# Input projections of a hybrid block's mixer in one stage of seven-product pairs, with results through DRAM and the recurrent branch's output projection beside attention

## The chip, the cores and the metric

The kernel runs on one core of a Trainium2 chip. The metric is the device time in microseconds of one execution. A core has a matrix engine (PE, with its own weight loads, PEld), a vector engine (DVE), a scalar engine (ACT), a general engine (POOL) and a sync engine (SP) that mostly issues DMAs. All of them share an on-chip memory (SBUF); PE writes to PSUM banks, from which DVE and ACT read; DMA queues move data to and from the memory outside (DRAM).

## The reference

One layer with width 1024, sequence 1024, batch 1: a half feed-forward (ffn1), a mixer, another half feed-forward (ffn2), each behind a norm and a modulation computed from a vector `c`. The change is in the mixer.

```python
def mixer(h, w_in, rel_bias, conv_w, conv_b, lru_wa, lru_ba, lru_wx, lru_bx, lru_lambda,
          w_att_o, w_rec_o, w_out):
    proj = h @ w_in
    q, k, v, xr, yr, g_att, g_rec = jnp.split(proj, idx, axis=-1)   # widths 512 x 3, 1024 x 4
    att = chunked_attention(q, k, v, rel_bias) @ w_att_o            # 8 heads of 64, own chunk + 8 before
    xr = causal_depthwise_conv(xr, conv_w, conv_b)                  # width 4
    rec = (rg_lru(xr, lru_wa, lru_ba, lru_wx, lru_bx, lru_lambda) * jax.nn.gelu(yr)) @ w_rec_o
    merged = jax.nn.sigmoid(g_att) * att + jax.nn.sigmoid(g_rec) * rec
    return merged @ w_out
```

`rg_lru` computes two gates by block-diagonal products, from them a decay `a` and an input `u`, and the recurrence h(t) = a(t) h(t-1) + u(t) along the sequence.

## The kernel before, in words

Everything is kept transposed: 128 channels on the partitions, 1024 positions along the free axis. A float32 product is made of three matmuls on split operands (high by high, high by low, low by high), so each operand is first cut into a high half (a cast on ACT) and a low half (a subtraction on DVE, or on POOL); `split` does that for weights. A projection of 128 columns over 1024 inputs and 1024 positions takes 48 matmuls of 512 columns.

In ffn1 and ffn2 most pairs of column groups (gate and up) go through seven products instead of eight, in the manner of Strassen and Winograd: the eight half-size products of two 128-column groups, each over two halves of the inputs, become seven over mixed operands, 84 matmuls instead of 96. `mix` makes the mixed weights: sums on POOL (L611), the high half on ACT (L623), the low half on DVE (L624). Sums of the moving operand are made once (`sum_step`, `differences`). `block` runs the products in the order 1, 2, 6, 5, 7, 3, 4 into three banks (`psX`, `psY`, `psZ`); after each, ACT copies a bank or DVE adds it (`vec`, L643).

The mixer has four phases after ffn1.
- `lru_phase`: for each of eight groups b, direct products for xr and yr, the convolution (three DVE operations, L1042), the GELU of yr, the gates' matmuls, the decay, one POOL product (L1090), the scan on DVE (L1091), and the split of the result, which stays in SBUF as `rec_h`, `rec_l`. Its matmuls are followed by those of the next group, in an order that the framework's scheduler sets.
- `rec_out_phase`: for each n the gate `gr` and the product with `w_rec_o`; the result goes to DRAM (`part`). Beside it runs background work (`bg`): the modulation vector's columns for later, summed on DVE from 512 KB pieces of `w_ada` (L203).
- `att_phase`: PE's order is fixed by hand, unit by unit (4 head pairs p x 2 heads x 8 query blocks, 64 units). For each unit come `scores` (sc), the softmax on DVE and ACT (L1344 maximum, L1347 its negation, L1348 exp, L1349 reciprocal, L1350 scaling), the transposes (`ptr`), their split (`tt`, ACT L1362, DVE L1363), and the product with v (`pvo`), gathered by L1386 to L1390. Between these PE gets `filler`: the projections of the next pair's q and k, half of v, and the gate `ga`, 192 matmuls of 512 columns (or their worth) per pair, dealt out in proportion to `SHARE` by the width of the unit's window. `GATES` says how many of the `ga` columns each pair takes.
- `merge_phase`: the product with `w_att_o`, the two gated branches added. Then `out_phase`.

## Time and profile before

| | us |
|---|---|
| Median of 3 runs | 2229.1 (2227.11 to 2230.41) |
| The profiled execution | 2231.5 |
| Its span, first to last instruction | 2229.6 |
| Beside it (2231.5 - 2229.6) | 1.9 |

In the profile a line number such as L624 is that of the kernel file. A row of a group has the engine, the operation, output and inputs by the program's names, shapes and a count; then either "busy us, mean ns" and the idle time before it with what ended that, or the least, median and greatest duration in ns. The table of stages has, for a window of time, its length and then for PE, PEld, DVE, ACT and POOL the busy time with the number of instructions, the granted clock of PE as a share of full speed, the busy share of the DMA engines and what they moved. In the list of waits a row says which engine and line waited for which, for how long in all, how many times, and the longest. In this execution ffn1's pairs run until about 700 us, the recurrence beside x and y to 946, gates and rec out to 1104, q, k and half of v to 1151, attention to 1422, the merge to 1466.

### The profile page before, as it was taken

Reading aid. Unit: us, or ns where it says so; the run is one execution under the profiler, and the core shown is the slowest. Engines: PE = TensorE matmul, PEld = TensorE weight load, DVE = VectorE, ACT = ScalarE, POOL = GpSimd, SP = SyncE. Lnnn points to the kernel's source line nnn. Section 1 sums busy time; section 2 is a strip of 40 time slices with the busy share of each in tenths; the row PEclk is TensorE's granted clock in tenths of the full one; section 3 lists DMA queues with packets and bytes.
Section 4 is the critical chain, followed back from the end, with each engine's and each line's share of the span. In section 5 each row is a group of like instructions: output and inputs, shape, how many; then the busy total and the mean of one; then the engine's idle time right before and its main releaser. Section 6 shows DMA issues by size and latency. Waiting matters only on the chain. (4 is left out here: it accounts for less than half of the span.)

```text
span 2229.6 us, 26752 instructions
## 1 busy us (share of the span) xinstructions
PE 2156.7 (97%) x9963; PEld 1785.0 (80%) x9963; DVE 1332.4 (60%) x1696; ACT 1016.1 (46%) x1567; POOL 758.2 (34%) x538
## 2 busy tenths in 40 slices
PE   5999999999999999999999999999999999999998
PEld 3878788888877788888898988887788788888877
DVE  6686676558356677655336666545866564544456
ACT  3533333334446678721147777436443333334443
POOL 3458885422104111100021120005658793522102
PEclk9999999999999999999999999999999999999999
DMA  9437674459575111166412011464357653348374
GB/s 294 113 120 268 226 272 153 151 183 336 182 240 184 50 50 42 57 221 221 155 40 68 26 55 54 146 199 142 110 181 263 229 209 126 113 155 275 117 230 176
DMA packets 269595, 358.36 MB, mean 161 GB/s; under 512 B 16625, under 2 KB 178585, under 8 KB 269465
## 3 DMA queue, kind: packets, MB, share of 16 engines
q1 hardware_dynamic: 256680, 310.48, 43.0%
q10 hardware_dynamic: 12784, 46.18, 5.4%
q8 instruction: 78, 1.28, 0.2%
q14 instruction: 53, 0.43, 0.1%
HBM read 265.37 MB, written 94.37 MB: 161 GB/s over the span
## 5 line engine op out<-in xcount | busy, mean ns | idle before, releaser
L624 DVE TENSOR_TENSOR wm<-raw,wm 128x512 fp32r<-128x512 f32 x152 | 161.0, 1063 | 165.3 <-ACT wm L623 162.5
L143 ACT CAST dh<-rawd 128x1024 fp32r<-128x1024 f32 x154 | 161.3, 1053 | 212.1 <-PE pv L882 67.0
L144 DVE TENSOR_TENSOR dh<-rawd,dh 128x1024 fp32r<-128x1024 f32 x130 | 161.9, 1250 | 153.4 <-ACT dh L143 145.3
L455 PE MATMUL pj<-hh,wl 128*128 128x512 f32 x576 | 228.3, 396 | 6.3 <-DVE wl L144 4.1
L454 PE MATMUL pj<-hl,wh 128*128 128x512 f32 x576 | 228.5, 397 | 5.7 <-DVE hl L336 5.7
L453 PE MATMUL pj<-hh,wh 128*128 128x512 f32 x576 | 230.9, 401 | 2.8 <-ACT h L344 1.9
L882 PE MATMUL px<-dh,dh 128*128 128x512 f32 x608 | 187.8, 390 | 1.7 <-DVE dh L144 1.7
L882 PE MATMUL pv<-dh,dh 128*128 128x512 f32 x528 | 164.3, 393 | 3.0 <-DVE dh L144 3.0
L325 POOL TENSOR_SCALAR rstd<-rstd 128x1 f32<-128x1 f32 x47 | 31.7, 675 | 392.5 <-ACT junk L324 390.9
L144 POOL TENSOR_TENSOR wl<-raw,wh 128x1024 fp32r<-128x1024 f32 x25 | 61.1, 2450 | 297.8 <-ACT wh L143 252.0
L143 ACT CAST wh<-raw 128x1024 fp32r<-128x1024 f32 (+1 forms) x86 | 86.7, 1010 | 144.9 <-DMA raw<-in_w_in_dram 41.8
L820 POOL TENSOR_TENSOR act<-act,act 128x512 f32<-128x512 f32 x54 | 87.5, 1620 | 158.9 <-DMA act<-act 89.1
L882 PE MATMUL px<-dh 128*128 128x512 f32 x352 | 137.9, 392 | 0.0
L455 PEld LDWEIGHTS pj<-hh,wl 128*128 128x128 f32 x576 | 110.2, 191 | 31.2 <-DVE wl L144 5.7
L882 PEld LDWEIGHTS px<-dh,dh 128*128 128x128 f32 x608 | 113.8, 188 | 26.5 <-DVE dh L144 3.0
L454 PEld LDWEIGHTS pj<-hl,wh 128*128 128x128 f32 x576 | 110.0, 191 | 29.9 <-DVE hl L336 7.6
L453 PEld LDWEIGHTS pj<-hh,wh 128*128 128x128 f32 x576 | 110.2, 191 | 26.2 <-ACT h L344 2.3
L144 DVE TENSOR_TENSOR wl<-raw,wh 128x1024 fp32r<-128x1024 f32 (+1 forms) x61 | 73.9, 1212 | 84.8 <-ACT wh L143 84.8
L633 PE MATMUL psX<-hh,wm 128*128 128x512 f32 x296 | 116.4, 393 | 4.3 <-ACT mixes L656 4.3
L882 PEld LDWEIGHTS pv<-dh,dh 128*128 128x128 f32 x528 | 99.5, 189 | 25.0 <-DVE dh L144 4.3
L633 PE MATMUL psX<-hs,wm 128*128 128x512 f32 x296 | 115.9, 391 | 1.6 <-ACT mixes L649 1.4
L623 ACT CAST wm<-raw 128x512 fp32r<-128x512 f32 x152 | 92.6, 613 | 52.1 <-POOL raw L611 52.0
(311 smaller groups left out, 5783.9 us busy)
## 6 DMA issues: line engine op xcount, KB each, us to landing
rawa<-in_w_ada_dram SPq DMA_DIRECT2D x56, 512.0 KB, 4.5
raw<-in_ffn_w_gu_dram SPq DMA_DIRECT2D x49, 512.0 KB, 4.7
rawd<-acts SPq DMA_DIRECT2D x88, 256.0 KB, 4.3
rawd<-downs SPq DMA_DIRECT2D x88, 256.0 KB, 4.1
raw<-in_w_in_dram SPq DMA_DIRECT2D x44, 512.0 KB, 4.0
sr<-in_ffn_w_gu_dram SPq DMA_DIRECT2D x39, 512.0 KB, 6.3
act<-act SPq DMA_DIRECT2D x37, 512.0 KB, 5.1
acts<-act ACTq DMA_DIRECT2D x36, 512.0 KB, 3.6
```

What stands on the lines that cost most here:

```text
L143: nc.scalar.copy(hi, raw)
L144: (eng or nc.vector).tensor_tensor(lo, raw, hi.bitcast(F32), op=ALU.subtract)
L325: nc.gpsimd.tensor_scalar(r, r, eps, None, op0=ALU.add)
L453: nc.tensor.matmul(dst, wh[:, kk, :], xhk[:, sl], start=first, stop=False)
L454: nc.tensor.matmul(dst, wh[:, kk, :], xlk[:, sl], start=False, stop=False)
L455: nc.tensor.matmul(dst, wl[:, kk, :], xhk[:, sl], start=False, stop=last)
L623: nc.scalar.copy(t[:, 0], src)
L624: nc.vector.tensor_tensor(t[:, 1], src, t[:, 0].bitcast(F32), op=ALU.subtract)
L633: nc.tensor.matmul(dst, t[:, 0, kk, :], xh, start=first and kk == 0, stop=False, skip_group_check=True)
L820: nc.gpsimd.tensor_tensor(o, p, q, op=op)
L882: nc.tensor.matmul(dst, a_[:, 0, tk], w_[:, 1, :], start=first and n == 0, stop=last and n == 2, skip_group_check=True,)
```

## The change: what it does

`seven` is cut out of `ffn`, with its sums, mixes and products unchanged, so that the mixer can use it. `lru_phase`, `rec_specs`, `rec_out_phase`, and the projections inside `att_phase` go; a `mixer_phase` takes their place, which computes all input projections. Its order is written by hand for all four compute engines. It starts with two direct `gr` columns and v, beside which the sums and the first mixes are made. Then come 19 blocks of seven products: xy0, gr, xy1, gr, xy2, gr, xy3, ga, xy4, ga, xy5, ga, xy6, ga, xy7, and q with k for the four head pairs. After each product, `after` makes one mix of the next block, and takes one step of the recurrence (`lru_steps`, a generator) and one of the gates' or q and k's conversion (`gate_steps`, `qk_steps`), and after three of the seven one step of the background work.

```diff
+        def block(n, after):
+            ...
+            run(1, chain, True)
+            nc.scalar.copy(u, chain)
+            after(1)
+            run(2, b2, True)
+            vec(u, b2, u)
+            after(2)
+            run(6, chain, False)
+            nc.scalar.copy(v, chain)
+            after(6)
+            b3 = bank("psZ")
+            run(5, b3, True)
+            nc.scalar.copy(pp, b3)
+            after(5)
+            run(7, chain, False)
+            vec(pp, chain, pp)
+            after(7)
+            run(3, b3, False)
+            vec(v, b3, v)
+            after(3)
+            run(4, chain, False)
+            if kind in ("gr", "ga"):
+                nc.scalar.activation(low, chain, AF.Tanh, scale=0.5)
+            else:
+                nc.scalar.copy(low, chain)
+            after(4)
+            return row0, row1
...
+        def lru_steps(b, xr, y):
...
+            nc.scalar.activation(q, q, AF.Sqrt)
+            yield
+            nc.gpsimd.tensor_tensor(ti, ti, q, op=ALU.mult)
+            yield
+            nc.vector.tensor_tensor_scan(q, a, ti, 0.0, op0=ALU.mult, op1=ALU.add)
+            nc.vector.tensor_tensor(q, q, g, op=ALU.mult)
+            rh = t4("rh", F32R)
+            nc.scalar.copy(rh, q)
+            yield
+            nc.vector.tensor_tensor(q.bitcast(F32R), q, rh.bitcast(F32), op=ALU.subtract)
+            yield
+            for i, src in enumerate((rh.bitcast(F32), q)):
+                nc.sync.dma_start(rec_d[i, b * P : (b + 1) * P, :], src)
+            yield
...
+                def after(i):
+                    sv.mix(n + 1, i)
+                    for q in (heavy, light):
+                        if q and next(q[0], BANK) is BANK:
+                            q.pop(0)
+                    if i in (2, 5, 3):
+                        bg(1)
```

The results go to DRAM: the recurrence's high and low halves (`rec_d`, 8 MB), q and k (`qk_d`), v (`v_d`), and the gates (`tgr`, `tga`). `att_phase` loads them again with DMAs issued by POOL, and its filler is now the product with `w_rec_o`, two column groups (96 matmuls) per head pair. `merge_phase` loads its gate from DRAM as before, for all columns.

```diff
+            def load_rec():
+                hi = [hpool.tile([P, S], F32R, tag="h", bufs=16, name=nm("rh")) for _ in range(KB)]
+                lo = [hpool.tile([P, S], F32R, tag="h", bufs=16, name=nm("rl")) for _ in range(KB)]
                 for k in range(KB):
+                    for i, t in enumerate((hi[k], lo[k])):
+                        nc.gpsimd.dma_start(t, rec_d[i, k * P : (k + 1) * P, :])
...
             def filler(p):
-                for kind, n in plan[p]:
-                    ...
+                load_qk(p + 1)
+                yield from rec_out(2 * p)
+                load_v(p)
+                yield from rec_out(2 * p + 1)
 
             with tc.manual_schedule(engines={PE_ENGINE}):
                 load_bias(0)
-                for _ in qk(0, qkt):
-                    pass
+                load_qk(0)
+                load_rec()
+                load_v(-1)
                 pe_next = scores(units[0])
-                for _ in vproj(0, vts):
-                    pass
...
-                    rate = (weight_of(p) - (LEFT if p == 3 else 0.0)) / tot
+                    rate = (96.0 - (LEFT if p == 3 else 0.0)) / tot
```

How this stands in the engines' programs, at three places. A number behind a name is that of the buffer. First DVE around one scan of the recurrence. Before (`xc` convolution, `wl` the low half of a weight, `xcl` and `rl` low halves, `g` the GELU):

```order
L1089 SCALAR_TENSOR_TENSOR ti_6016<-ti_6016,xc_5694 128x1024
L1042 SCALAR_TENSOR_TENSOR xc_5987<-xr_5986,colsB,xc_5987 128x1021
L1087 SCALAR_TENSOR_TENSOR q_6097<-q_6097,tr_6015 128x1024
L1051 TENSOR_TENSOR xcl_5996<-xc_5987,xch_5995 128x512
L1051 TENSOR_TENSOR xcl_6000<-xc_5987,xch_5999 128x512
L1091 SCALAR_TENSOR_TENSOR q_6097<-a_6096,ti_6016 128x1024
L144 TENSOR_TENSOR wl_6191<-raw_6188,wh_6190 128x1024
L1064 TENSOR_SCALAR g_6090<-g_6090 128x1024
L1092 TENSOR_TENSOR a_6096<-q_6097,g_5905 128x1024
```

The same stretch of a scan in the change (`wm` low halves of the next block's mixes, `acc` the background sums, `row` with a `ps` bank the block's own sums):

```order
L1211 SCALAR_TENSOR_TENSOR ti_6561<-ti_6561,xc_6454 128x1024
L1110 TENSOR_TENSOR row_1006_6605<-psY_6608,row_1006_6605 128x512
L558 TENSOR_TENSOR wm_6648<-rawm_6601,wm_6648 128x512
L202 SCALAR_TENSOR_TENSOR acc_6328<-rawa_6573,c_act,acc_6328 128x1024
L558 TENSOR_TENSOR wm_6671<-rawm_6601,wm_6671 128x512
L1215 SCALAR_TENSOR_TENSOR q_6629<-q_6629,tr_6560 128x1024
L558 TENSOR_TENSOR wm_6691<-wsum_6622,wm_6691 128x512
L202 SCALAR_TENSOR_TENSOR acc_6328<-rawa_6655,c_act,acc_6328 128x1024
L1110 TENSOR_TENSOR row_1007_6606<-psX_6607,row_1007_6606 128x512
L558 TENSOR_TENSOR wm_6711<-rawm_6603,wm_6711 128x512
L1220 SCALAR_TENSOR_TENSOR q_6629<-a_6628,ti_6561 128x1024
L1221 TENSOR_TENSOR q_6629<-q_6629,g_6455 128x1024
```

Four mixes, two background sums and two sums of banks that PE waits for (`psY`, `psX`) stand now between the recurrence's steps, where the convolution and two low halves of the next group stood.

Second, POOL at the beginning of attention (`bw` is the bias table of the first head, loaded by SP). Before:

```order
L1090 TENSOR_TENSOR ti_7047<-ti_7047,q_7069 128x1024
L144 TENSOR_TENSOR wl_8371<-raw_8368,wh_8370 128x1024
L144 TENSOR_TENSOR wl_8377<-raw_8374,wh_8376 128x1024
L1308 MEMSET bw_8216 64x64
L1309 MEMSET bw_8216 64x64
L1308 MEMSET bw_8350 64x64
```

In the change:

```order
L1344 DMA k_9417<-qk_d 64x1024 x2
L1344 DMA k_9420<-qk_d 64x1024 x2
L1393 MEMSET bw_9401 64x64
L1394 MEMSET bw_9401 64x64
L1324 DMA rh_9423<-rec_d 128x1024
L1324 DMA rl_9431<-rec_d 128x1024
L1324 DMA rh_9424<-rec_d 128x1024
L1324 DMA rl_9432<-rec_d 128x1024
```

The loads of q and k of the first pair, then the two memsets of `bw`, then sixteen loads of the recurrence's halves, of which four are shown, and behind them the loads of v (`vt`). On SP the load of `bw` stands right behind the last four stores to `qk_d`, and its buffer lies where those stores read. `rh` and `rl` take the buffers of the mixer's moving operand (`hh`, `hl` and their sums).

Third, PE between the scores of two full units of attention. Before:

```order
L1228 MATMUL pj_9493<-hh_948,wl_9312 128x512
L1376 MATMUL pvo_9500<-tt_9454,vt_8434 128x256 x2
L1376 MATMUL pvo_9500<-tt_9454,vt_8486 128x256
L1358 MATMUL ptr_9504<-ident,pe_9424 128x128 x4
L1228 MATMUL pj_9493<-hh_949,wh_9311 128x512
L1228 MATMUL pj_9493<-hl_957,wh_9311 128x512
L1228 MATMUL pj_9493<-hh_949,wl_9312 128x512
L1228 MATMUL pj_9493<-hh_950,wh_9311 128x512
L1228 MATMUL pj_9493<-hl_958,wh_9311 128x512
L1228 MATMUL pj_9493<-hh_950,wl_9312 128x512
L1228 MATMUL pj_9493<-hh_951,wh_9311 128x512
L1339 MATMUL sc_9519<-k0h_8770,q_1315_8606 128x320
```

In the change:

```order
L1461 MATMUL pvo_10240<-tt_10214,vt_9455 128x256 x2
L1461 MATMUL pvo_10240<-tt_10214,vt_9456 128x256
L1443 MATMUL ptr_10244<-ident,pe_10187 128x128 x4
L1370 MATMUL pj_10236<-rh_9424,wh_9796 128x512
L1370 MATMUL pj_10236<-rl_9432,wh_9796 128x512
L1370 MATMUL pj_10236<-rh_9424,wl_9797 128x512
L1370 MATMUL pj_10236<-rh_9425,wh_9796 128x512
L1424 MATMUL sc_10256<-k_9496,q_9493 128x320
```

Between the transposes and the next scores stand four filler matmuls instead of seven, and their operands are the recurrence's halves from DRAM. Over the whole program PE has 228 matmuls of 512 columns fewer.

More of the change, by code (lines that the diff above doesn't have):

```diff
@@ L1287, in g_att @@
-            def g_att(n):
-                for sh in range(2):
-                    pj = yield from pproj(wts["ga", n], sh)
-                    tg = tmp[0].tile([P, 512], F32, tag="v", bufs=1, name=nm("tga"))
-                    nc.scalar.activation(tg, pj, AF.Tanh, scale=0.5)
-                    nc.sync.dma_start(tg_dram[n * P : (n + 1) * P, sh * 512 : (sh + 1) * 512], tg)
-                    yield 1.0
+                    if k == KB - 1:
+                        nc.vector.scalar_tensor_tensor(tg[:, sl], tg[:, sl], 1.0, dst[sh], op0=ALU.add, op1=ALU.mult)
+                        yield 1.0
@@ L1486, in merge_phase @@
             nc.sync.dma_start(pr, part[n * P : (n + 1) * P, :])
-            if i + 1 < KB:
-                nxt = gate(order[i + 1])
+            if n + 1 < KB:
+                nxt = gate(n + 1)
             pa = proj(wts["ao", n], att_h, att_l, n=4)
```

607 lines of the change are left out of this document (306 added, 301 removed).

## The prediction

> **What bounds the kernel now.** I read the page first, for who is busy over the whole span.
>
> ```profile
> span 2229.6 us, 26752 instructions
> PE 2156.7 (97%) x9963; PEld 1785.0 (80%) x9963; DVE 1332.4 (60%) x1696; ACT 1016.1 (46%) x1567; POOL 758.2 (34%) x538
> ```
>
> PE is the bound: 97% busy, so removed matmuls are worth their time unless something else becomes the limit where they stood. That is asked of a table by stage: PE, PE load, DVE, ACT, POOL, granted clock, DMA share and rate.
>
> ```profile
> core 0: us, PE busy (x) PEld busy (x) DVE busy (x) ACT busy (x) POOL busy (x), PEclk, DMA share, GB/s
> 140.00:480.00 340.00, 333.92 (x1460) 272.75 (x1459) 221.19 (x254) 122.49 (x218) 228.88 (x154) 1.00 0.60 204
> 760.00:946.00 186.00, 186.00 (x822) 154.04 (x821) 136.15 (x125) 146.69 (x184) 21.59 (x14) 1.00 0.18 51
> 946.00:1104.00 158.00, 158.00 (x713) 130.78 (x712) 75.03 (x76) 27.91 (x35) 2.39 (x1) 1.00 0.62 200
> 1126.00:1151.00 25.00, 25.00 (x204) 24.76 (x203) 4.18 (x10) 7.53 (x13) 4.65 (x5) 1.00 0.08 22
> 1151.00:1422.00 271.00, 264.23 (x1531) 230.14 (x1530) 163.53 (x444) 191.83 (x390) 42.06 (x38) 1.00 0.16 50
> 1422.00:1466.00 44.00, 43.79 (x193) 36.33 (x194) 29.44 (x35) 11.89 (x14) 0.00 (x0) 1.00 0.79 256
> ```
>
> The rows are: ffn1's seven-product blocks, the recurrence beside x and y, gates and rec out, half of v, attention, merge. PE never lacks work from 760 to 1151 and lacks 6.8 us in attention. One matmul of 512 columns takes 186.00/822 = 0.2263 us. The other engines are far from full: DVE 136 of 186 us beside the recurrence, ACT 192 and DVE 164 of 271 in attention. The change puts more of their work against less of PE's.
>
> **Term 1, products removed.** Nineteen pairs take 84 matmuls instead of 96. 19 x 12 x 0.2263 = **-51.6 us**. The other matmuls (two direct gate columns, v, the recurrence's 96, rec out's 384, attention) only move. The new blocks run at the clock of 1.00 that all rows show.
>
> **Term 2, the mixer blocks.** A block has 84 matmuls, 19.0 us; where the recurrence's gate products stand, up to 12 more, 2.7 us. Blocks 1 to 16, which carry recurrence, have 16 x 84 + 96 = 1440 matmuls, 326 us. The prices of DVE's work in them:
>
> ```profile
> L624 DVE TENSOR_TENSOR wm<-raw,wm x152: 675/789/1825, 132.8 to 1984.5; 128x512 fp32r<-128x512 f32 x152
> L624 DVE TENSOR_TENSOR wm<-sr,wm x70: 675/1058/1766, 155.7 to 1986.0; 128x512 fp32r<-128x512 f32 x70
> L624 DVE TENSOR_TENSOR wm<-wsum,wm x37: 679/1536/1789, 140.7 to 1978.2; 128x512 fp32r<-128x512 f32 x37
> L643 DVE TENSOR_TENSOR pp<-psX,pp x37: 676/691/692, 155.1 to 1998.9; 128x512 f32<-128x512 f32 x37
> L203 DVE SCALAR_TENSOR_TENSOR acc<-rawa,c_act,acc x49: 1269/1284/3461, 320.0 to 1060.7; 128x1024 f32<-128x1024 f32 x49
> L1042 DVE SCALAR_TENSOR_TENSOR xc<-xr,colsB,xc 128x1023 f32<-128x1023 f32 x8 | 10.3, 1282 | 8.4 <-ACT xc L1033 8.4
> L1087 DVE SCALAR_TENSOR_TENSOR q<-q,tr 128x1024 f32<-128x1024 f32 x8 | 9.8, 1225 | 5.3 <-ACT q L1086 5.3
> L1064 DVE TENSOR_SCALAR g<-g 128x1024 f32<-128x1024 f32 x8 | 5.5, 686 | 0.0
> L1091 DVE TENSOR_TENSOR_SCAN q<-a,ti 128x1024 f32<-128x1024 f32 x8 | 18.3, 2292 | 28.1 <-POOL ti L1090 28.1
> L1090 POOL TENSOR_TENSOR ti<-ti,q 128x1024 f32<-128x1024 f32 x8 | 19.2, 2403 | 82.3 <-ACT q L1088 82.3
> L611 POOL TENSOR_TENSOR raw<-wsum,raw x37: 1272/1293/1744, 137.6 to 1974.2; 128x512 f32<-128x512 f32 x37
> ```
>
> Two neighbouring blocks (one recurrence) need: 14 mixes x 0.68 = 9.5; `vec` sums 6 x 0.69 = 4.1; the recurrence 3 x 1.28 + 0.69 + 7 x 1.22 + 2.29 + 0.42 = 15.8; modulation sums, which filled the roomy rec-out stage before (DVE 75 of 158 us) and now stand in the blocks, 28 in the 16 blocks, 3.5 x 1.28 = 4.5. That is 33.9, or 271 us for 16 blocks, and 276 with two last products of the modulation and the first q and k low halves, free of contention.
>
> The three mix rows show contention: the same operation takes 675 ns at best but 789, 1058 and 1536 in the median, beside a POOL that is busy 229 of 340 us; the weighted mean is 0.97 us, 1.43 times the best. The sums read from PSUM stay at 691. In the new blocks POOL has 8 x 1.29 + 2.4 + 0.4 = 13.1 us in about 41, or 32% instead of 67%: a factor of 1 + 0.43 x 32/67 = 1.2 on all but the 40 us of PSUM sums and single-input work. DVE: 236 x 1.2 + 40 = **324 us against PE's 326**. The trace has no stage where DVE is that full.
>
> Three costs follow. Work is uneven over blocks: counting each block's instructions in the new order by these prices, DVE exceeds PE in eleven blocks, by 13.6 us together. PE gives nothing back, since the products' banks alternate and PE waits for `pp` with one product's slack (2.7 us). The scan stands right behind its POOL operation (2.4 us), and DVE already idles 28.1/8 = 3.5 us ahead of each; with DVE the late engine that is about 2.5 us for seven scans, less some slack, 15 us. The prelude's sums and first mixes add some 5. **+33 us.** Bounds: +5 if DVE overlaps as in ffn1 (DVE 221 of 340 us, PE short by 6.1), +75 if half of DVE's free third in that stage (119/340 x 1/2 x 19 = 3.3 us a block, 18 blocks, on top of 14) stays idle here through waits.
>
> [...]
>
> ACT gains copies of chains and q, k conversions but falls below DVE's load; table loads stay at 19. DMA is at most 3 MB a block, 160 GB/s, below the 204 beside which ffn1's PE ran, so I price these stores and weight loads at nothing; the cover is the two-block lead of the weight loads.
>
> **Term 3, the load before attention.** Before, q and k of pair 0 came straight from PSUM. Now they, v and the recurrence come by DMAs that POOL issues. `rh`, `rl` take the slots of `hh`, `hl`, so none of the 16 can start before PE's last products. In POOL's order the two memsets of `bw` stand ahead of them, `bw`'s load waits for space held by the last q/k stores, and the first `vt` is the 17th DMA behind; PE's first `pvo` wants it, with eight rec products ahead of it. The prices:
>
> ```profile
> L1084 ACT ACTIVATE a<-tr,sp_cm 128x1024 f32<-128x1024 f32 x8 | 10.2, 1278 | 0.0
> acts<-act ACTq DMA_DIRECT2D x36, 512.0 KB, 3.6
> bw<-relrep SPq DMA_DIRECT2D x8, 320.0 KB, 3.4
> POOL bw L1308 <- DMA bw<-relrep: 6.1, 2, 5.5
> ```
>
> From PE's last product: copy 0.7 (as a 640-wide cast takes below), high half 1.3, low half 1.3, store 3.6, `bw` 3.4, memsets 0.3: 10.6 us. Then 17 x 512 KB = 8.9 MB. The merge row moves 256 GB/s at a share of 0.79, so full engines would move 324: 27.5 us. PE fills about 3 of it. **+35 us.** Bounds: +22 if the first 10.6 hides (the slots come free 2.7 us before the end) and +47 if the loads run at merge's 256 GB/s, 7 us more, and issuing adds 5. The trace has no DMA issued by POOL. [...]
>
> **Term 4, attention with half the filler.** Before, each head pair carried 192 matmuls of projections, now 96 of rec out. The chain of one full unit against the next:
>
> ```profile
> L1348 ACT ACTIVATE pe<-pe,nmx 128x640 f32<-128x640 f32 x32 | 26.6, 831 | 28.0 <-DVE nmx L1347 27.6
> L1348 ACT ACTIVATION_READ_ACCUMULATOR pe<-pe,nmx 128x1 f32 x64 | 12.0, 187 | 0.0
> L1362 ACT CAST tt<-ptr 128x640 fp32r<-128x640 f32 x32 | 21.9, 686 | 2.6 <-PE ptr L1358 2.2
> L1363 DVE TENSOR_TENSOR tt<-ptr,tt 128x640 fp32r<-128x640 f32 x32 | 26.3, 823 | 20.4 <-ACT tt L1362 20.0
> L1344 DVE CUSTOM_DVE_ANT_0 pe<-sc,bw 128x640 f32<-128x640 f32 x32 | 26.2, 818 | 2.5 <-PE sc L1339 2.2
> L1344 DVE DVE_READ_ACCUMULATOR2_ANT mx<- 128x1 f32 x64 | 5.2, 82 | 0.1
> L1347 DVE TENSOR_SCALAR nmx<-mx 128x1 f32<-128x1 f32 x64 | 9.7, 151 | 1.7
> L1376 PE MATMUL pvo<-tt,vt 128*128 128x256 f32 x240 | 40.3, 288 | 4.3 <-DVE tt L1363 4.2
> L1387 DVE TENSOR_TENSOR o<-o,pvo 64x256 f32<-64x256 f32 x32 | 13.4, 419 | 10.9 <-ACT o L1386 10.7
> L1388 DVE TENSOR_TENSOR o<-o,pvo 64x256 f32<-64x256 f32 x32 | 13.3, 416 | 0.8
> L1390 DVE TENSOR_TENSOR attl<-o,atth 64x256 fp32r<-64x256 f32 x31 | 17.5, 566 | 0.9 <-ACT atth L1389 0.2
> ```
>
> ACT does exp of the next unit, then `tt` of this one; DVE the low half of `tt`, then the next scores and their maximum, for which the next exp waits: 0.83 + 0.19 + 0.69 + 0.82 + 0.82 + 0.08 + 0.15 = 3.58 us. Half of the output sums on DVE ((0.42 + 0.42 + 0.57)/2 = 0.70 a unit) gives 3.93. PE's share: attention before, less its 672 projection matmuls and the v half (25.0), is 264.2 - 152.1 - 25.0 = 87 us; it goes with the width, and a full unit has 5 of the 240 column blocks: 1.82 us. The filler, handed out by shares (5 of 67), is 96/67 x 5 x 0.2263 = 1.62. So 3.44 us in the first three pairs, 2.77 in the last, where 40 matmuls are kept back. 24 x 0.49 + 8 x 1.16 = 21; the shorter units, by an estimate, 4; less the 6.8 idle before: **+18 us.** Bounds: 0, if units overlap enough that only the sums count (ACT's and DVE's own work there adds to some 170 and 153 us, PE's to 174), +45 with all output sums and the short units in the chain.
>
> **Sum.** -51.6 + 33 + 35 + 18 = +34. The profiled execution took 2231.5 us (span and 1.9 around it), 2.4 above the median, so **2263 us** on the median's scale. All low ends give 2204, all high ends 2344.
>
> **Rivals.** (1) The other side: DVE keeps up, as it did beside the recurrence (136 of 186 us, PE never short), and units overlap in attention. Terms 2 and 4 are then 5 and 0: -51.6 + 35 + 5 = -12, 2217 us. It decides where the two fall under 17 us together; against it stands 324 against 326. (2) The load is short, at its low bound of 22: 2250; for it speaks that the last pair's conversions may precede PE's end. [...]
>
> **Chances.** The forecast 0.45, with its own range 2241 to 2287; rivals 0.20, 0.12, 0.23. The range runs from 2214 to 2320, leaving out the corners where all ends agree. A difference of 0.2% (4.5 us) is about what a measurement tells from no change. Rival 1 gives most of faster, 0.19; 0.06 within; 0.75 slower.
>
> **What would show it.** By stage in the changed trace: DVE over 85% busy in the blocks while PE waits for `row1`/`wm` from DVE, some 33 us; PE idle once for about 35 us behind `vt`, `rh` DMAs; attention 25 us above PE's busy time, waits of `ptr` and `pvo` for ACT and DVE. The forecast is wrong if DVE shows long idle with PE full in the blocks, or if the rec loads start before `bw`'s memsets end.

## The result and the profile after

The change makes the kernel slower: 2356.4 us against 2229.8 for the kernel before on the same chip, a ratio of 1.0566 (95% interval 1.0548 to 1.0585), or +126.6 us. The forecast was 2263, its range ended at 2320, and the sign alone was right.

The page of the kernel after, its first lines:

```profile
span 2353.2 us, 27010 instructions
PE 2152.8 (91%) x9735; PEld 1762.3 (75%) x9735; DVE 1485.7 (63%) x1859; ACT 1054.8 (45%) x1652; POOL 909.7 (39%) x667
```

PE has 228 matmuls fewer (9735 against 9963), and was busy only 4 us less: many of them took longer. The table by stage (length, then PE, PEld, DVE, ACT, POOL busy, granted clock, DMA share and rate); the rows are everything up to the mixer, the direct columns and v, the 19 blocks, the gap, attention, the merge, and the rest:

```profile
0.00:757.00 757.00, 716.24 (x3197) 586.73 (x3198) 485.98 (x567) 313.03 (x463) 344.00 (x241) 0.99 0.62 205
757.00:795.00 38.00, 38.00 (x305) 37.42 (x304) 32.10 (x37) 13.76 (x23) 18.98 (x9) 1.00 0.22 76
795.00:1255.00 460.00, 417.73 (x1732) 334.27 (x1731) 352.15 (x350) 252.44 (x367) 154.01 (x99) 0.95 0.44 141
1255.00:1305.00 50.00, 6.40 (x16) 4.07 (x16) 4.80 (x15) 8.24 (x15) 15.32 (x32) 0.58 1.06 325
1305.00:1548.00 243.00, 191.54 (x1041) 157.05 (x1041) 149.72 (x423) 148.77 (x319) 34.61 (x54) 0.93 0.43 104
1548.00:1590.00 42.00, 41.83 (x184) 34.66 (x185) 25.85 (x31) 9.35 (x12) 0.00 (x0) 1.00 0.80 256
1590.00:2353.00 763.00, 741.06 (x3265) 608.13 (x3263) 435.14 (x440) 309.22 (x456) 342.80 (x234) 0.99 0.53 180
```

The mixer and the merge took 709 us before (757 to 1466) and take 833 now; outside them nothing moved (763 us from the merge's end in both). The matmul records give the parts: each matmul's start to the next is set against the pitch that its width had before (0.227 us for 512 columns, 0.146 for 320, 0.120 for 256, 0.109 for 128); what is more counts as waiting if PE stood idle between, as slow clock if not.

| stage | length | matmuls at before's pitch | PE waits | slow clock |
|---|---|---|---|---|
| 19 blocks | 460 | 389 | 46 | 23 |
| gap | 50 | 3 | 45 | 2 |
| attention | 243 | 168 | 58 | 15 |
| direct columns and v, merge | 80 | 79 | 0 | 0 |
| before, all of the mixer | 709 | 694 | 8 | 4 |

So 55 us of matmuls went, and some 177 us of waits and slow clock came. Who PE waited for in the kernel after (waiting line, releasing line: us in all, times, longest):

```profile
PE pvo L1461 <- DVE tt L1448: 23.2, 19, 7.0
PE ptr L1443 <- ACT pe L1435: 18.7, 10, 13.4
PE pvo L1461 <- DMA vt<-v_d: 16.2, 1, 16.2
PE sc L1418 <- DVE mx L1429: 14.0, 1, 14.0
PE psZ L567 <- ACT row L1126: 13.3, 5, 6.3
PE psX L567 <- DVE row L1110: 10.3, 6, 3.6
PE psX L567 <- ACT row L1122: 9.2, 4, 4.6
PE sc L1418 <- DMA k<-qk_d: 9.0, 2, 6.9
```

Rows with `psZ` and `psX` are in the blocks, `sc` and `vt` in the gap, `pvo <- tt` and `ptr` in attention. A stretch of PE's row in time, in block 12, counted from 0 (start, duration, in brackets the idle time ahead):

```profile
1092.54 0.39 PE L569 MATMUL psZ<-hs,wm 128*128 128x512 f32 x1
1094.45 0.51 PE L452 MATMUL pgate<-xh,gw 128*128 128x512 f32 x1 [1.53 <-ACT gw L1192]
1095.41 0.56 PE L453 MATMUL pgate<-xl,gw 128*128 128x512 f32 x1 [0.45 <-DVE xl L1193]
1096.82 0.80 PE L454 MATMUL pgate<-xh,gw 128*128 128x512 f32 x1 [0.85 <-DVE gw L1194]
...
1099.12 0.63 PE L568 MATMUL psX<-hl,wm 128*128 128x512 f32 x1
1099.55 0.63 PE L569 MATMUL psX<-hh,wm 128*128 128x512 f32 x1
1099.98 0.63 PE L567 MATMUL psX<-hh,wm 128*128 128x512 f32 x1
```

Three waits of 2.8 us together are followed by matmuls 0.43 us apart (1099.12, 1099.55, 1099.98) instead of 0.23, until 1102. That is the slow clock in the table: in the blocks 121 matmuls come more than 0.1 us late without a wait. The granted clock's record has eleven stretches at 0.50 there, of 3.4 or 6.8 us each. The prediction, which read a clock of 1.00 in every row before and kept it, had no such term.

### The profile page after: what moved, and what is told of

It is laid out like the page before. It is cut to its first block, busy times and chain, and to the rows that moved or that the text cites. A ratio compares the mean times of both kernels' runs of the same rounds, so it can differ in the third digit from the quotient of the medians.

```text
span 2353.2 us, 27010 instructions
## 1 busy us (share of the span) xinstructions
PE 2152.8 (91%) x9735; PEld 1762.3 (75%) x9735; DVE 1485.7 (63%) x1859; ACT 1054.8 (45%) x1652; POOL 909.7 (39%) x667
## 3 DMA queue, kind: packets, MB, share of 16 engines
q8 instruction: 76, 1.25, 0.2%
## 5 line engine op out<-in xcount | busy, mean ns | idle before, releaser
L567 PE MATMUL psX<-hs,wm 128*128 128x512 f32 x448 | 178.4, 398 | 13.7 <-DVE row L1110 10.3
L567 PE MATMUL psX<-hh,wm 128*128 128x512 f32 x448 | 178.3, 398 | 13.3 <-ACT row L1122 9.2
L568 PE MATMUL psX<-hl,wm 128*128 128x512 f32 x448 | 176.8, 395 | 0.0
L569 PE MATMUL psX<-hs,wm 128*128 128x512 f32 x448 | 176.6, 394 | 0.0
L569 PE MATMUL psX<-hh,wm 128*128 128x512 f32 x448 | 176.6, 394 | 0.0
L568 PE MATMUL psX<-hs,wm 128*128 128x512 f32 x448 | 176.3, 394 | 0.0
L558 DVE TENSOR_TENSOR wm<-rawm,wm 128x512 fp32r<-128x512 f32 x114 | 103.8, 914 | 65.2 <-ACT wm L557 60.5
L545 POOL TENSOR_TENSOR wsum<-rawm 128x512 f32<-128x512 f32 x19 | 28.1, 1481 | 235.3 <-DMA rawm<-in_w_in_dram 202.6
L567 PEld LDWEIGHTS psX<-hs,wm 128*128 128x128 f32 x448 | 85.6, 191 | 37.4 <-DVE row L1110 13.5
L567 PEld LDWEIGHTS psX<-hh,wm 128*128 128x128 f32 x448 | 85.8, 192 | 34.3 <-ACT row L1122 10.9
L887 PE MATMUL pv<-dh 128*128 128x512 f32 x264 | 104.0, 394 | 3.7 <-ACT dh L142 3.7
```

The costliest lines, as they stand in the source:

```text
L545: nc.gpsimd.tensor_tensor(out, p, q, op=op)
L558: nc.vector.tensor_tensor(t[:, 1], src, t[:, 0].bitcast(F32), op=ALU.subtract)
L567: nc.tensor.matmul(dst, t[:, 0, kk, :], xh, start=first and kk == 0, stop=False, skip_group_check=True)
L568: nc.tensor.matmul(dst, t[:, 0, kk, :], xl, start=False, stop=False, skip_group_check=True)
L569: nc.tensor.matmul(dst, t[:, 1, kk, :], xh, start=False, stop=last and kk == 3, skip_group_check=True)
L887: nc.tensor.matmul(dst, a_[:, 0, tk], w_[:, 1, :], start=first and n == 0, stop=last and n == 2, skip_group_check=True,)
```

## The experiments: the mixer's blocks

The first idea was order: ACT, in front of the copies that PE waits for, itself waits for DVE (52 us ahead of `rh`, 24 ahead of `xh` in the blocks). Three runs moved the recurrence's steps without changing any engine's work.

**e1.** ACT's waiting instructions one step later.

```diff
             nc.vector.tensor_tensor(q, q, g, op=ALU.mult)
             rh = t4("rh", F32R)
+            yield
             nc.scalar.copy(rh, q)
             yield
```

> The changed kernel with the recurrence's steps cut in another way: ACT's high half of the convolved input, its square root and its high half of the result each come one step behind the DVE instruction that they wait for, instead of in the same step; as many steps as before. Theory O (order: in the mixer blocks PE waits for bank copies that stand on ACT behind an instruction which waits for DVE; DVE's own load, 77% of the stage, is not the limit): ACT's waits on DVE of 52 us (result) and 24 us (convolution) mostly go, the blocks fall from 460 to about 415 us, the kernel from 2356 to about 2310. Theory D (DVE with POOL beside it is simply too full, as the prediction had it): DVE's work is the same, no more than 10 us go, 2346 or above.

Measured 2363.2 us, ratio 1.0590 (1.0574 to 1.0606): nothing gained. The steps for `xh` and the square root moved in the same way, which put `xl` one step nearer to the gates' matmuls, and PE's weight loads now wait for it for 22 us.

**e5.** The same steps at other products of the block.

```diff
-                    for q in (heavy, light):
-                        if q and next(q[0], BANK) is BANK:
-                            q.pop(0)
-                    if i in (2, 5, 3):
+                    for _ in range({6: 0, 5: 0, 3: 2, 4: 2}.get(i, 1)):
+                        for q in (heavy, light):
+                            ...
+                    if i in (1, 2, 3):
                         bg(1)
```

> The changed kernel with the same steps called at other products of a block: none of the recurrence's or the gates' steps after products 6 and 5, two each after 3 and 4, and the background's three steps after 1, 2 and 3. Theory S (slots: between the copies that PE waits for after products 6 and 5, and before the sum that it waits for after 7, ACT and DVE get more than a product's 2.7 us of other work in some blocks, so PE waits; the copies were late in 32 cases or so): PE's waits of 46 us and the slow clock behind them fall by half or more, blocks 460 to about 420, the kernel 2356 to about 2315. Theory D (DVE's load as a whole): nothing, 2350 to 2360.

Measured 2372.0, ratio 1.0637 (1.062 to 1.0655), 16 us worse than the change (a difference between the two ratios to the kernel before, as in what follows), and outside both forecasts. PE's wait for the copy after 5 went from 13.3 us to 1.7; the wait for the copy after 1 rose from 1.9 to 21.3, for the copy after 6 from 9.2 to 16.3, and for the gates' weights from 3.5 to 14.1.

**e9.** Two groups in turn, so that dependent steps stand two products apart (with e1's cut).

```diff
                         if q and next(q[0], BANK) is BANK:
                             q.pop(0)
+                        elif q is heavy and len(q) > 1:
+                            q[0], q[1] = q[1], q[0]
```

> The changed kernel with two groups of the recurrence in turn: after each product still one step is taken, but of two generators alternately, so that a step and the one that depends on it stand two products (5.4 us) apart instead of one; ACT's three waiting instructions are one step later than the DVE work they need, as in the run on that, and the GELU's result goes into its input's buffer. The load of every engine is the same. Theory L (latency: the recurrence is one chain through DVE, ACT, POOL and PE, each step stands in order one product behind the step that it needs and passes its lateness on to the copies that PE waits for): the blocks fall from 460 to about 420 us, the kernel to about 2315. Theory D (DVE's load): nothing, 2350 to 2360.

Measured 2364.5, ratio 1.0600 (1.0573 to 1.0628). It did what it was made for: PE no longer waits for ACT's copies, with 6 us left in the list below. But it waits for DVE instead:

```profile
PE psX L567 <- DVE row L1110: 35.3, 10, 9.6
PE pgate L453 <- DVE xl L1194: 8.7, 5, 3.0
PE psZ L567 <- ACT row L1126: 5.7, 3, 3.6
```

None of the three orders gained anything, so order and latency alone are not shown to be the cause; other orders were not tried. The next runs left the order as it was and changed what the engines have to do.

**e12.** The recurrence left out.

```diff
         def lru_steps(b, xr, y):
+            yield
+            for i, src in enumerate((xr, y)):
+                nc.sync.dma_start(rec_d[i, b * P : (b + 1) * P, :], src)
+            return
```

> The changed kernel with the recurrence's steps left out (convolution, GELU, gates, scan; x and y go to DRAM in place of the result's halves), so that between the products only mixes, sums, gates, q and k and the background stand; 96 matmuls, 22 us of PE, are left out too. If the blocks of seven products by themselves lose time (their three banks and one product of slack, as beside ffn1, where PE waits for 6 us in 340): the blocks stay 20 us or more above their 367 us of matmuls. If the recurrence's steps between them cause the waits, be it by load or by latency: within 8 us of 367, so the kernel at 2356 - 22 - 65 = 2269.

Measured 2260.5, ratio 1.0145 (1.0128 to 1.0162). The blocks take 370 us for 368 of matmuls. The seven products themselves lose 2 us; the recurrence between them costs the rest of the 71 us that the change's blocks take above their matmuls.

**e2.** Three quarters of the background's sums left out.

```diff
-        for k in range(KB):
+        for k in range(few[0]):   # 2 in the mixer's blocks
             if raw_home[0] == "t4":
```

> The changed kernel with the background's sums for the modulation cut from eight pieces to two in each of its four jobs in the mixer, so 24 DVE instructions (1.39 us each in the profile, 33 us) and 12 MB of loads are left out. Theory D: the blocks get shorter by what DVE saves, some 30 us, 2325. Theory O: DVE idles for ACT anyway, so a half of it or less comes out: 2340 to 2350.

Measured 2342.1, ratio 1.0495 (1.0478 to 1.0513): 16 us of 32 that DVE has less. That is the range forecast for order, and a miss for DVE's load by itself; the waits below show why.

**e13.** POOL's sums of weights left out.

```diff
             def pool(out, p, q, op):
-                nc.gpsimd.tensor_tensor(out, p, q, op=op)
+                if sums_on:
+                    nc.gpsimd.tensor_tensor(out, p, q, op=op)
```

> The changed kernel without POOL's sums of weights in the mixer's blocks (four per block, 76 of 128x512; the mixes then cut the unsummed weights). DVE's, ACT's and PE's work is the same by count. DVE's mixes take 0.92 us in the blocks against 0.68 at best, its convolution 1.5 to 1.7 against 1.28. Theory P (POOL beside DVE, by the contention and by POOL's place in the chain ahead of each mix, fills DVE): DVE's 352 us in the blocks fall to about 305 and the blocks by 25 us or more, 2330 or below. Theory A (ACT is the one that the others wait for: DVE waits 72 us for its mixes): within 8 us of 2356.

Measured 2313.5, ratio 1.0373 (1.0357 to 1.039): 43 us less than the change, the largest step of any run that keeps PE's work.

**e15.** The recurrence's DVE instructions on half of the columns.

```diff
-            nc.vector.tensor_tensor_scan(q, a, ti, 0.0, op0=ALU.mult, op1=ALU.add)
-            nc.vector.tensor_tensor(q, q, g, op=ALU.mult)
+            nc.vector.tensor_tensor_scan(q[:, hf], a[:, hf], ti[:, hf], 0.0, op0=ALU.mult, op1=ALU.add)
+            nc.vector.tensor_tensor(q[:, hf], q[:, hf], g[:, hf], op=ALU.mult)
```

> The changed kernel with the recurrence's in-place DVE instructions on half of the columns (the second half of the sequence is left out there): same instructions, order and waits, but some 60 us less of DVE's 352 in the blocks. Theory D (DVE is too full, 352 of the 389 us that the matmuls need, and it waits in order besides): blocks from 460 to about 415, the kernel to about 2312. Theory A or order alone (which engine waits for which, not how long DVE works): within 15 us of 2356.

Measured 2318.8, ratio 1.0403 (1.0387 to 1.0418): 36 us less.

**e16.** ACT's part lighter.

```diff
-            nc.scalar.activation(q, q, AF.Sqrt)
+            nc.scalar.activation(q[:, 0:512], q[:, 0:512], AF.Square)
```

> The changed kernel with ACT's part lighter: a square in place of the square root, so that 16 of 19 table loads (1.28 us each) go, and three of the recurrence's in-place functions and the gates' on half of the columns: some 45 us less of ACT's 252 in the blocks, DVE's work the same. Theory A: blocks fall by 30 us or more, 2325 or below. Theory D: no more than 15 us, 2341 or above.

Measured 2348.5, ratio 1.0534 (1.0515 to 1.0553): 7 us less. The stage rows of the blocks of the change, e16, e2, e13, e15 and e12, in this order:

```profile
794.83:1254.80 459.97, 417.90 (x1734) 334.44 (x1732) 352.32 (x350) 252.45 (x366) 154.18 (x99) 0.95 0.44 141
792.38:1248.27 455.89, 412.13 (x1734) 330.08 (x1732) 352.87 (x350) 217.25 (x344) 157.46 (x99) 0.97 0.44 142
795.94:1246.67 450.73, 411.08 (x1734) 330.18 (x1732) 320.39 (x326) 252.01 (x366) 150.79 (x99) 0.97 0.35 116
790.74:1210.02 419.28, 401.91 (x1734) 325.51 (x1732) 308.32 (x347) 248.24 (x358) 30.63 (x25) 0.98 0.47 154
794.61:1224.91 430.30, 402.39 (x1734) 323.96 (x1732) 304.04 (x350) 252.99 (x366) 141.62 (x99) 0.98 0.46 151
792.52:1162.85 370.33, 368.25 (x1638) 304.31 (x1636) 210.69 (x246) 137.24 (x239) 120.35 (x85) 1.00 0.54 176
```

The third figure of each row after its length is DVE's. With DVE at 352 us the blocks take 460 or 456, whether ACT has 252 us or 217; at 320, 451; at 308 and 304, 419 and 430; at 211, 370 (and 22 us fewer matmuls). So DVE sets the blocks' pace, though it is at most 77% busy. Its busy time alone does not give the length: e2 takes 32 us from it and only 9 from the blocks. The other part is DVE's wait for ACT's high half of each mix, here of the change, e2, e13 and e12:

```profile
DVE wm L558 <- ACT wm L557: 72.4, 46, 6.3
DVE wm L559 <- ACT wm L558: 90.9, 52, 6.3
DVE wm L561 <- ACT wm L560: 79.5, 53, 3.4
DVE wm L558 <- ACT wm L557: 110.1, 67, 6.0
```

Busy time and this wait together are 425 us in the change, 426 in e16 (waiting 73), 411 in e2, 388 in e13 and 395 in e15 (waiting 91), and the blocks are 30 to 39 us longer each time. In e12 they are 321, below the 368 of the matmuls, and the wait, though longer, costs PE next to nothing. In the change only 37 us of the matmuls' 389 are spare beside DVE's 352, so a wait of 72 cannot be made up. e15 also shortens the recurrence's own chain, which no run separates from DVE's load. Between e13 and e15, with DVE alike, e13 is 11 us shorter; there POOL also no longer stands ahead of the mixes. DVE's rows in the blocks, of the change and of e13 (mean ns behind the bar):

```profile
L558 DVE TENSOR_TENSOR wm<-rawm,wm 128x512 fp32r<-128x512 f32 x112 | 102.6, 919 | 65.2 <-ACT wm L557 60.5 <-PE pc L216 4.7
L1220 DVE TENSOR_TENSOR_SCAN q<-a,ti 128x1024 f32<-128x1024 f32 x8 | 20.4, 2551 | 0.0
L1110 DVE TENSOR_TENSOR row<-psZ,row 128x512 f32<-128x512 f32 x19 | 13.0, 686 | 6.4 <-PE psZ L569 6.3
```

```profile
L561 DVE TENSOR_TENSOR wm<-rawm,wm 128x512 fp32r<-128x512 f32 x130 | 100.1, 773 | 79.7 <-ACT wm L560 79.5
L1223 DVE TENSOR_TENSOR_SCAN q<-a,ti 128x1024 f32<-128x1024 f32 x8 | 18.2, 2280 | 0.0
L1113 DVE TENSOR_TENSOR row<-psZ,row 128x512 f32<-128x512 f32 x19 | 13.0, 686 | 4.6 <-PE psZ L572 4.5
```

Without POOL's sums the mixes' low halves fall from 919 to 773 ns and the scan from 2551 to 2280, while the sum with a PSUM operand stays at 686. DVE's time in the blocks falls by 44 us. Of these rows the two that are slower beside POOL's sums have two inputs in SBUF, the third has one there and one in PSUM; whether the inputs' place is the reason, no run separates. An operation of the GELU with a single input in SBUF (`g<-g`) took 684 ns in the median of its eight in the change, once 1779, and 686 in the kernel before, where POOL was busy for 22 of the stage's 186 us.

## The experiments: the loads before and in attention

**e3.** POOL's loads no longer behind the bias table.

```diff
-                nc.gpsimd.memset(bw[0:HD, 576:640], NEG)
-                nc.gpsimd.memset(bw[HD:P, 0:HD], NEG)
+                nc.vector.memset(bw[0:HD, 576:640], NEG)
+                nc.vector.memset(bw[HD:P, 0:HD], NEG)
```

> The changed kernel with the two memsets of the bias table on DVE instead of POOL, so that POOL's loads of the recurrence do not stand behind the table's load. Theory G (the gate: the loads of the recurrence start 24 us after PE's last product because POOL waits for the table): they start some 20 us earlier and the gap of 50 us falls to about 35, the kernel to about 2340. Theory B (bytes: the DMA queues are full, at a share of 1.06 and 325 GB/s, from PE's last product to the first product with v, so whatever is issued earlier takes turns with the loads of q and k and the last stores): the gap stays within 5 us, 2351 to 2356.

Measured 2351.0, ratio 1.0538 (1.0514 to 1.0563). The loads of the recurrence start at 1262 us instead of 1279, but the first product with v at 1300 instead of 1305.

**e19.** Half of the recurrence's bytes.

```diff
-                    for i, t in enumerate((hi[k], lo[k])):
-                        nc.gpsimd.dma_start(t, rec_d[i, k * P : (k + 1) * P, :])
-                recs.update(hi=hi, lo=lo)
+                    nc.gpsimd.dma_start(hi[k], rec_d[0, k * P : (k + 1) * P, :])
+                recs.update(hi=hi, lo=hi)
```

> The changed kernel with only the high halves of the recurrence loaded before attention, used in place of the low ones too, so 4.2 MB less ahead of v, with POOL's order and waits as they were. Theory B (bytes at the rate of some 325 GB/s that full queues give set PE's gap of 50 us): the first product with v starts 10 to 13 us earlier and the kernel takes about 2345. If the gate (the bias table's load, then latency of each load) sets it: no more than 5 us.

Measured 2347.1, ratio 1.0526 (1.0504 to 1.0548): 9 us less. The first product with v, of the change, e3 and e19 (the last two figures are its first and last start):

```profile
L1461 PE MATMUL pvo<-tt,vt x240: 274/282/582, 1305.0 to 1544.3; 128*128 128x256 f32 x120
L1461 PE MATMUL pvo<-tt,vt x240: 274/283/582, 1300.2 to 1539.4; 128*128 128x256 f32 x120
L1459 PE MATMUL pvo<-tt,vt x240: 274/282/582, 1294.0 to 1531.6; 128*128 128x256 f32 x120
```

Starting the loads 17 us earlier gave 5 us; 4.2 MB less, at the same order, gave 11. The gap's row above has the queues at a mean share of 1.06 and 325 GB/s, so 16 MB in 50 us. In 40 slices of 1.25 us, from 1255 to 1305 in the change (busy tenths, then the rate):

```profile
DMA  9999999999999995285079999999999999999999
GB/s 360 377 283 243 242 227 220 262 235 236 242 298 417 419 419 213 50 274 223 7 242 374 347 347 288 390 416 419 419 419 416 413 410 406 413 413 406 410 410 406
```

Bytes set most of the gap, but not at one rate: some 240 GB/s while the stores and loads of q and k share the queues, and 406 to 419 for the recurrence and v at the end, at which 4.2 MB are 10 us. Around 1274 to 1281 the queues run half empty, while POOL's loads stand behind the bias table; the 5 us of e3 are of that size. Why the first stretch is slower was not tried.

**e4.** v first.

```diff
                 load_qk(0)
-                load_rec()
                 load_v(-1)
+                load_rec()
```

> The changed kernel with the four loads of v ahead of the sixteen of the recurrence, so that the first product with v needs 2.5 MB (one piece of v and four of the recurrence stand ahead of it on PE, and three more of v in the queue) instead of 8.9. Theories G and B alike: the gap shrinks from 50 to about 35 us, and some of it comes back as PE's filler then waits for the rest of the recurrence: 2340 to 2350. If the attention units that run meanwhile hide the loads in full, 2335.

Measured 2345.9, ratio 1.0512 (1.0487 to 1.0536).

A gain of 12 us, as both theories had it; the first product with v starts at 1295.

**e6.** q and k of the next pair later.

```diff
-                load_qk(p + 1)
                 yield from rec_out(2 * p)
+                load_qk(p + 1)
                 load_v(p)
```

> The changed kernel with the loads of the next pair's q and k (3 MB) behind the first of the two rec-out products of a pair instead of ahead of it. If the stall of 13 us at 1337 us of the changed kernel (ACT waits 12.9 us for a piece of w_rec_o that takes 13.2 us to land among the other loads, PE waits for ACT's scaling) comes from the bytes in flight, it goes: 2340 to 2346. If that piece is late for its place in the sync engine's queue, it stays: 2354 to 2358.

Measured 2341.3, ratio 1.0500 (1.0484 to 1.0516): the bytes in flight. ACT's long wait falls from 12.9 to 0.9 us, while a second one grows from 5.3 to 7.4. The two in the change (start, duration, idle ahead); each stands ahead of the softmax in ACT's queue, and PE waits 13.4 and 7.0 us behind them:

```profile
1349.46 1.04 ACT L142 CAST wh<-raw 128x1024 fp32r<-128x1024 f32 x1 [12.88 <-DMA raw<-in_w_rec_o_dram]
1406.21 1.04 ACT L142 CAST wh<-raw 128x1024 fp32r<-128x1024 f32 x1 [5.30 <-DMA raw<-in_w_rec_o_dram]
```

**e11.** e6, and w_rec_o's pieces two products ahead (`ahead=1` becomes `ahead=2`).

> The run with q and k of the next pair later, and w_rec_o's pieces asked for two products ahead instead of one. There ACT still waits 7.4 us for such a piece at 1399 us, ahead of the softmax work in its queue, and PE has long waits in two units (13.2 and 8.0 us). If these are that piece coming late: some 10 us less than that run, 2330. If they are the bytes in flight alone or something else: within 4 us of its 2341.

Measured 2336.2, ratio 1.0482 (1.0467 to 1.0498). Inconclusive between its two forecasts: ACT still waits 7.1 us for a piece, and PE 8.8 behind it.

**e8.** Loads paced, pair 0's filler on its second head.

```diff
                     share = rate * SHARE[window(u[2])[1] - 1]
+                    if u[0] == 0:
+                        share *= 67.0 / 31.0 if u[1] else 0.0
```

> The changed kernel with v's loads ahead of the recurrence's, the bias table's memsets on DVE, q and k of the next pair later (as in the run on that alone), and pair 0's filler dealt out over its second head only, so that the first eight units need nothing of the recurrence while its 8 MB land. Theory B (bytes before the first product with v set the gap): PE's gap falls from 50 to about 25 us, and with the stall of 13 us gone too the kernel ends near 2315. If the wait only moves into the first eight units (chain of 3.9 us a unit without filler, and then the recurrence's loads): 2335 to 2345.

Measured 2343.8, ratio 1.0517 (1.0499 to 1.0535): the second case. The first product with v starts at 1297, and PE then waits once for 24.9 us ahead of an early unit's scores: the wait moved.

**e18.** All edits to the loads but that pacing (e3, e4, e6, e11).

> The changed kernel with all edits to the loads before and in attention at once: v ahead of the recurrence, the bias table's memsets on DVE, q and k of the next pair later, w_rec_o's pieces two products ahead. The mixer's blocks are not touched. If the gains of the single runs (10, 5 and 20 us) add up: 2321. If they take turns at the same full DMA queues: 2328 to 2336. Neither comes near the kernel before.

Measured 2329.0, ratio 1.0445 (1.0419 to 1.0472): 27 us, so the gains do not add up. It is the fastest run of the changed kernel that leaves none of the work out, and 99 us slower than the kernel before. No version that beats the kernel before was found; even without any recurrence (e12) it was not beaten.

**e7.** The kernel before with halved filler, no result through DRAM.

```diff
-GATES = (2, 0, 2, 4)
+GATES = (0, 0, 0, 2)
```

> The kernel before with the gate projections of attention's filler moved out into the merge, all but two for the last head pair: pairs 0, 2 and 3 then have 96 matmuls of filler as in the changed kernel, pair 1 still 192, and no result goes through DRAM. PE's work is the same. Theory C (the chain of a unit through ACT and DVE, 3.9 us against PE's 3.4 and 2.8, sets attention's pace once the filler is halved): some 17 to 25 us more, 2247 to 2256. If units overlap enough: within 5 us of 2230, and attention's loss in the changed kernel is its loads alone.

Measured 2272.5, ratio 1.0196 (1.0181 to 1.0212): 43 us, about twice the forecast. Its waits of PE, and the row of its attention, which ends near 1398, with some of the gate products that were moved behind it:

```profile
PE pvo L1376 <- DVE tt L1363: 14.2, 15, 2.7
PE pvo L1376 <- DVE nmx L1347: 13.5, 9, 4.5
PE ptr L1358 <- ACT pe L1350: 4.8, 8, 1.2
1151.00:1440.00 289.00, 253.47 (x1421) 214.63 (x1421) 168.17 (x452) 188.32 (x384) 28.44 (x32) 0.96 0.13 40
```

By the count of the first table its attention has 40 us of waits and 14 of slow clock, where the kernel before has 7 and 4. In the change, of 58 and 15, some 20 us of waits are the two stalls behind weights. The rest, 38 and 15, is close to e7's 40 and 14, so to what halved filler costs by itself, though e7 halves it in only three of the four pairs.

**e10 and e17.** Matmuls that nobody needs, in the gap.

```diff
                 pe_next = scores(units[0])
+                warm = bank("warm")
+                for _ in range(260):
+                    nc.tensor.matmul(warm[:, 0:P], ones_r, ones_r, start=True, stop=True)
```

> The changed kernel with 260 matmuls of 128 columns on a constant (28 us at full clock), whose results nobody reads, put on PE behind the first unit's scores, where PE idles for the loads. Theory K (PE's granted clock falls to about a half while it idles, and the matmuls behind an idle stretch take 0.43 instead of 0.23 us for some microseconds): the clock is near 1.00 when the loads have come, the matmuls of the first units after the gap take 0.23 us, and 3 to 6 us are gained. If the lower clock comes from the loads or from the kind of matmul instead, the first units run as slowly as before and the time stays or grows.

> The changed kernel with 120 matmuls of 512 columns (constant weights, q of the first pair as the moving operand; nobody reads the result), 27 us at full clock, behind the first unit's scores. With 128 columns the matmuls ran at 0.214 us each and the granted clock stayed at 0.50 for 52 us. If what keeps the clock down is that PE's array is mostly idle between short matmuls: the clock rises to 1.00 within some 5 us here and the first units behind the gap run at 0.23 us a matmul; the time is 2350 to 2356. If it is the loads, or the stage: it stays at 0.50 to 0.60, the matmuls end near 1320 us and the kernel takes about 2370.

e10 measured 2360.8, ratio 1.0596 (1.0578 to 1.0614); e17 2357.8, ratio 1.0574 (1.0555 to 1.0593). Rows of e10 and then of e17 in the gap (the granted clock is the third figure from the end):

```profile
1278.00:1300.00 22.00, 22.00 (x105) 22.00 (x105) 0.62 (x4) 2.18 (x4) 9.02 (x19) 0.50 0.91 316
```

```profile
1264.00:1270.00 6.00, 1.92 (x5) 1.60 (x6) 0.00 (x0) 0.00 (x0) 1.43 (x3) 0.50 1.28 229
1270.00:1280.00 10.00, 10.00 (x39) 7.96 (x39) 0.00 (x0) 1.05 (x1) 0.00 (x0) 0.88 1.10 313
1280.00:1300.00 20.00, 20.00 (x89) 16.11 (x88) 1.20 (x7) 2.63 (x6) 8.67 (x18) 1.00 0.93 322
```

Matmuls of 512 columns bring the clock to 1.00 within the second row; those of 128 columns, though PE is busy in every microsecond, leave it at 0.50. So in these two runs the clock goes with PE's work, not with the loads (a DMA share of 0.91 in e10's row at 0.50, of 0.93 in e17's at 1.00) or the stage (the moving operand differs too, a constant in e10 and q in e17). Neither run gained time, and e17 ends 2 us above the range of the case that its clock bears out: v came at its own time, and in the 8.5 us that PE then still waited for it (e17) the clock fell again, to 0.66 on average from 1300 to 1310.

## Why the prediction was wrong, point by point

**Term 1, -51.6 us: right.** 55 us of matmuls went by the table, which has ragged ends at its stages; the 12 matmuls per pair are gone.

**Term 2, +33 us; measured 69.** DVE's load was nearly right: 313 us in the 16 blocks that carry the recurrence, against 324, with POOL's part (44 us by e13) of the size that the factor of 1.2 gave. The failed step is "Three costs follow": from a load of 324 against 326 us it took only the unevenness, the scans and the prelude. In-order waits of DVE for ACT's high halves (72 us) were not priced, though a stage that full cannot absorb them. Of the 69, 23 are slow clock, for which the sum had no term at all; the upper bound of 75 was without it, so its nearness is in part luck. The sign that was to show the term did not appear as forecast: DVE was 77% busy, not over 85, and of PE's 42 us of waits in the blocks 24 ended with ACT's copies, which can stand behind ACT's own waits for DVE, and only 10 with DVE's sums. POOL's sums are the largest single part that a run shows, 43 us of the kernel's time by e13, but not all of it.

**Term 3, +35 us; measured 47.** The failed step is "From PE's last product", the 10.6 us ahead of the loads. The recurrence's first load started 24 us behind that product (1278.9 against 1254.6): 3 MB of q and k and 2 MB of last stores shared the queues, those stores took 16.2 us to land instead of the 3.6 used, and the bias table's load stood behind them. From there to the first product with v it took 26 us, where the sum had 27.5. That the mean rate of 325 GB/s is the 324 of the sum is luck, as the slices show.

**Term 4, +18 us; measured 62** (58 + 15 less 7 + 4), above its own bound of 45. The chain of one full unit at 3.93 us was somewhat long: full units start 3.3 to 3.7 us apart on average in pairs 2 and 3. The failed step is the sum "24 x 0.49 + 8 x 1.16 = 21; the shorter units, by an estimate, 4", which has none of three other costs: the two stalls of 20 us behind weights (a load that is late stands in ACT's queue ahead of the softmax), 11 us more of slow clock than before, and more at the short units. With the two stalls set aside, PE stands idle for some 17 to 20 us beside full units, near the 21, and for 11 to 13 beside short ones instead of 4.

**The sign** was right, with 0.75 on slower, and rival 1 (DVE keeps up) was wrong where it was to be decided, in the blocks. All three unknown terms came out high at once, and the range had left out "the corners where all ends agree"; even with all high ends the sum was 2344. The terms were not independent: behind PE's waits of 46 us in the blocks and 58 in attention came 23 and 15 us of slow clock.

## What to carry to other kernels

Work that is moved beside a saturated engine is priced by the second engine's busy time together with its in-order waits: here DVE with 352 us busy and 72 of waiting beside 389 of matmuls cost 71 us, and with 211 and 110 beside 368 it cost 2. Bytes that stand between two stages are summed up with everything in flight, stores too: here 16 MB in 50 us, where the sum had 8.9 MB of loads. And each removed stretch of filler that lets PE wait can be paid twice, once as the wait and once as the slow clock behind it, 58 and 15 us in this attention.

## What the runs showed of the hardware that was not expected

The record of PE's granted clock moves in steps of 3.41 us, and the matmuls of 512 columns behind a fall come every 0.43 us instead of 0.23; 40 us of this kernel's mixer are that. Between 750 and 1600 us of the change the clock fell to 0.50 behind 16 steps. In 15 of these PE had idled for 1.83 us or more, in one wait or several; in the 16th it idled 0.61 us and spent 1.84 on matmuls of one column. In the 197 steps that stayed at full clock it idled 1.69 us at most, and over the same stretch of the kernel before the one fall came behind 1.68 us and the other 247 steps idled 1.51 us at most. So in these two executions about half a step of idling, 1.7 to 1.8 us, went with a fall, not a whole one.

Back-to-back matmuls of 128 columns (e10, 243 recorded in 52 us, 0.214 us each) did not raise the clock in that time, while 512 columns (e17) did in less than 10. An estimate from these numbers gives a half too: if 512 columns take the 0.43 us that the change shows at a clock of 0.50, 128 would take 0.107, half of the 0.214 us between two of them. No run tests it.

The low halves of q and k (`row<-row,hi`, 128x1024) took 1.73 us on DVE with POOL's sums and 1.74 without, where the low half `xl<-xc,xh` of the same shape took 1.22; why was not tried.
